# A two-layer hybrid inference step: TensorE issues in the order of tracing in the RWKV mixer and in the last layer's first token group

## The chip, the cores and the metric

The kernel runs on one core of one Trainium2 chip. The metric is the device time of the program in microseconds (us). The engines are named as in the profile: PE is TensorE, DVE is VectorE, ACT is ScalarE, POOL is GpSimd, and SP issues most of the DMA transfers. Matrices are multiplied on PE into PSUM banks; the other engines read the banks and the on-chip buffers (SBUF).

## The reference

One inference step of a two-layer decoder with model width 1024. A prompt of 1024 tokens with 16 learned tokens ahead of it (1040 tokens), and 8 single decode tokens with states of their own, go through both layers:

```python
for i in range(2):
    hn = rmsnorm(h, norm_mix[i])
    out = conformer_conv(hn) if i % 2 == 0 else rwkv7(hn)
    h = h + out
    h = h + square(relu(rmsnorm(h, norm_mlp[i]) @ w_in[i])) @ w_out[i]     # 1024 -> 4096 -> 1024
y = rmsnorm(h, norm_final)
```

Layer 0 mixes tokens with a Conformer convolution, layer 1 with RWKV-7 time mixing of 16 heads of 64. Time mixing projects r, k, v and, through small bottlenecks, a decay w, a rate a and a gate g for each token, and then runs a recurrence over the tokens for each head, with a 64 x 64 state S:

```python
sa = einsum(S, -kk_t)
S  = S * w_t + outer(sa, kk_t * a_t) + outer(v_t, k_t)
y_t = einsum(S, r_t)
out = ((groupnorm(y) + sum(r * k * r_k) * v) * g) @ w_o
```

The outputs are y of the prompt and of the decode tokens and the layers' final states.

## The kernel before

**Layer 0** works on three token groups and is not touched by the change. **Layer 1's mixer** works on four token groups of 272, 256, 256 and 264 tokens (`for g in range(4)`, L1417), and each group goes through eight pairs `p` of heads (128 columns). For each pair `mixer_in` (L880) traces the projection of r (`pr`), the second halves of the bottlenecks (`l_g`, `l_w`, `l_a`), the projection of v (`pv`), and then the deferred `finish` of the pair before: transposes of v (`vt`), products of the tokens within 32-token blocks (`nn`, L998, written to DRAM as `d_n`) and the bonus (`pk`, L1014). Between them it traces the key projections (`pk`, `pn`) of the next group. A projection (L845) is 16 matmul records of the trace, which stand as 8 rows in the order of instructions: each fp32 matmul leaves two records.

**The recurrence** runs over 17 chunks: chunk 0 holds the 16 learned tokens, chunks 1 to 16 hold 64 tokens each, and chunks 1, 5, 9 and 13 are the first of the four token groups. `front(c)` prepares a chunk. Before chunks 0, 1, 5, 9 and 13 it calls `inverses`, which loads the products `d_n` as `ni`, inverts 32 x 32 triangular blocks for one or four chunks in 30 rounds of two VectorE instructions (L1127, L1128: `tt<-ni`, `ni<-ni,tt`), and stores them as `d_p`. Then it loads `xa` and `bk` (DRAM `d_ab`) and the inverses `p32`, lets PE form the products of all tokens of the chunk (`A`, L1168, four banks) and DVE mask them (L1175, L1176), and transposes `p32` into `x32` on DVE (L1182). `chunk(c)` then does, on PE, `gg` (L1206, 32 x 32 tiles), the transposes `bT` (L1229), `W` (L1236), `po` (L1206), `U` (L1252), `S` (L1261) and `Y` (L1268, L1271), with copies and small products on the other engines between them, and updates the state `sv`. `bk` has one buffer, `xa` two. So `gg` of chunk 0 waits for this chain: `nn` of the last pair, DRAM, 60 DVE instructions, DRAM, `x32`.

**How the two are woven.** While the mixer of a group is traced, `tick` is called at every pair and in the projections; each call gives a credit, and `advance` traces steps of the recurrence until the credit is used up; the steps' prices stand in a table (`RW`). So the place of a recurrence step in the *program* is set by these credits. The place in which an engine *issues* it is set by something else: the whole program is ordered by a planner, which runs the instructions through a time model of its own and for each engine takes, of those that its model holds ready, the first in program order. An engine then executes its instructions strictly in that order, each behind the semaphores it needs.

**The last layer's stage** handles three token groups of 328, 352 and 352 tokens. For the first, `mixer_out(0)` multiplies the gated output by w_o (`ps_oo`), and `mlp(1, [group 0])` does the MLP: `ps_in` and `out`, with `h` and `r` on DVE behind them. These dense matmuls are split in three (L187, L188, L189: high by high, high by low, low by high parts). Into this stage a `filler` weaves what is left of the recurrence (chunks 13 to 16), the decode tokens' step (`decode_step`: 16 rounds of nine DVE instructions) and `norm_gate`, which transposes and gates the recurrence's output. The second and third token groups follow, with the same MLP.

PSUM is shared by name: four banks for the dense matmuls, one for small sums, and three ("w") for all steps of the recurrence.

Of the kernel before, what the change touches and what calls it, by code (L numbers as in the profile page):

```python
# [28 lines left out]
NCH = 1 + SEQ // HS  # L29
# [10 lines left out]
GN_OF = [[i for i, (lo, n) in enumerate(GN) if a <= lo < a + w] for a, w in G2]  # L40
# [8 lines left out]
def hybrid_step(tc, x_prompt, x_sample, state_conv, state_shift, state_wkv, meta_tokens,  # L49
# [8 lines left out]
    nc = tc.nc  # L58
    ctx = ExitStack()
    with ctx:  # L60
# [308 lines left out]
        with ExitStack() as l0:  # L369
# [6 lines left out]
            actp = [pool(l0, f"actp0{i}", 1) for i in range(2)]  # L376
            residp = [pool(l0, "resid00", 1)]
# [253 lines left out]
            with ExitStack() as s:  # L631
# [3 lines left out]
                fill, rest = filler(8 * KT, ([ranked(CV0, conv(0)), ranked(CV0, ln_silu(0))], EARLY * (15 * KT // 2 + 2 + 2 * MW + KT)))  # L635
# [6 lines left out]
                for g in range(3):  # L642
                    nxt, tail = iter(()), ()
                    if g < 2:
                        if g:
                            acts.append(new_act(actp[1], "hn2", N0))
                        nxt, tail = filler(TX, ([transpose_x(g + 1, *acts[g + 1])], 4 + 2 * KT))
# [202 lines left out]
        def keys(g, fill):  # L850

            c0, n = G1[g]
            nm = lambda s, *a: f"{s}{g}" + "".join(f"_{x}" for x in a)
            mix = prep[g][0]
            act = [mix(2, k) for k in range(KT)]
            pn = bank(nm("pn"), "x")
            add_pn = lambda: None

            def to_pn(p, sq):
                return lambda: nc.tensor.matmul(pn[:, :n], head_sel(p), sq[:, :n], start=p == 0, stop=p == KT - 1)  # L860
            for p in range(KT):
                yield
                ps = proj(next(wrkv), act, n, nm("k", p), fill)
                k_ = pr.tile([P, N1], F32, name=nm("st", p), tag="st", bufs=2)
                nc.scalar.copy(k_[:, :n], ps[:, :n])
                nc.sync.dma_start(d_k[:, p, c0:c0 + n], k_[:, :n])
                sq = pr.tile([P, N1], F32, name=nm("sq", p), tag="rk", bufs=2)
                nc.scalar.activation(sq[:, :n], ps[:, :n], AF.Square, scale=vec("k_k", p))
                add_pn()
                add_pn = to_pn(p, sq)  # L870
            r16 = lorap.tile([P, N1], F32, name=nm("r16"), tag="lf")
            r16p = norm[g] = [lorap.tile([P, N1], F32R, name=nm("r16" + q), tag="r16" + q, bufs=2)[:, :n] for q in "hl"]
            add_pn()
            nc.vector.tensor_scalar(r16[:, :n], pn[:, :n], L2_EPS * L2_EPS, None, op0=ALU.max)
            nc.scalar.activation(r16[:, :n], r16[:, :n], AF.Sqrt)
            nc.vector.reciprocal(r16[:, :n], r16[:, :n])
            split(*r16p, r16[:, :n], nc.vector)
# [432 lines left out]
        def advance(wait, last):  # L1310

            st["credit"] += wait
            while st["credit"] > 0 and st["done"] < last:
                w = next(rec)
                if w is None:
                    break
                st["credit"] -= w
            st["credit"] = min(st["credit"], 0)
# [93 lines left out]
        def tick(g, slow):  # L1412

            advance(PACE[g] * slow, NCH - 1)
            next(ng0, None)

        for g in range(4):  # L1417
            if g == 0:
                for _ in prepare(0):
                    pass  # L1420
                for _ in keys(0, lambda: None):
                    pass
            mixer_in(g, lambda slow=1.0: tick(g, slow))
        carry["tail"]()
        advance(CHUNK_WAIT * NCH, NEED[GN_OF[0][-1]])
        for _ in ng0:
            pass
        ld.close()


        with ExitStack() as l1:
# [10 lines left out]
            def mixer_out(g, residp, actp, fill, add):  # L1442
                lo, n = G2[g]
                h1 = hl[g] = residp.tile([P, KT, cur["wide"]], F32, name=f"h1_{g}", tag="h")
                nc.sync.dma_start(h1[:, :, :n], d_h[:, :, lo:lo + n])
                z = new_act(actp, f"z{g}", cur["wide"])
                for p in range(KT):
                    t = tt(f"zr{g}{p}", "t1")
                    nc.sync.dma_start(t[:, :n], d_z[:, p, lo:lo + n])
                    split(z[0][:, p, :n], z[1][:, p, :n], t[:, :n], nc.vector)  # L1450
                for m in range(KT):
                    ps = dense(load_col(rwkv_w_o[0], m, f"wo{g}_{m}", nc.gpsimd), z, n, f"oo{g}_{m}", fill)
                    nc.vector.tensor_add(h1[:, m, :n], h1[:, m, :n], ps[:, :n])
                    add(m, h1[:, m, :n])
                    fill()
# [57 lines left out]
            def group(g, actp, hidp, sums):  # L1513
                n = G2[g][1]
                hv = hl[g][:, :, :n]
                return (g, hv, n, *mlp_in(actp, hv, n, 1, f"m1{g}", sums), hidp)
# [4 lines left out]
                                ([until(NCH - 1)], FA * CHUNK_WAIT * (NCH - 1 - st["done"])),  # L1521
                                ([decode_step(), norm_gates(GN_OF[1]), ng2], NGA))
            add, sums = sums_of(0)
            mixer_out(0, residp, actp, fill, add)
            mlp(1, [group(0, actp, hidp, sums)], 2, nc.gpsimd, nc.vector, fill)
            for _ in rest:
                pass
            lw.close()
            outp = pool(l1, "outp", 1)
            cur["wide"] = max(n for lo, n in G2[1:])  # L1530
# [55 lines left out]
```

## Time and profile before

| | us |
|---|---|
| three runs | 2887.63, 2895.84, 2894.62 |
| median | 2894.62 |
| profiled execution | 2896.42 |
| its span | 2894.7 |
| mean granted clock of PE | 0.971 of full speed |

The span is cut by events of the trace into: layer 0 up to the mixer's first projection, `pk_0`, at 1124.2 us; the mixer with chunks 0 to 12, to its last `nn` at 1838.5; the mixer output with chunks 13 to 16 and the decode step, to about 2028; the rest of group 0's MLP, to 2313.3; and groups 1 and 2, to the end. In a row of PE events the columns are start, duration, engine, line, operation, output and inputs by the program's names (chunk and pair numbers left out), the tile of the array in use (128*128 is the whole array), the output's shape, and how many records the row joins; in square brackets stands how long the engine idled before it and what ended that.

### The profile page before, as it was taken

Reading aid. Unit: us, or ns where it says so; the run is one execution under the profiler, and the core shown is the slowest. Engines: PE = TensorE matmul, PEld = TensorE weight load, DVE = VectorE, ACT = ScalarE, POOL = GpSimd, SP = SyncE. Lnnn points to the kernel's source line nnn. Section 1 sums busy time; section 2 is a strip of 40 time slices with the busy share of each in tenths; the row PEclk is TensorE's granted clock in tenths of the full one; section 3 lists DMA queues with packets and bytes.
Section 4 is the critical chain, followed back from the end, with each engine's and each line's share of the span. In section 5 each row is a group of like instructions: output and inputs, shape, how many; then the busy total and the mean of one; then the engine's idle time right before and its main releaser. Section 6 shows DMA issues by size and latency. Waiting matters only on the chain.

```text
span 2894.7 us, 51574 instructions
## 1 busy us (share of the span) xinstructions
PE 2781.4 (96%) x19594; PEld 2573.7 (89%) x19594; DVE 1785.7 (62%) x3618; ACT 1187.1 (41%) x2233; POOL 1436.8 (50%) x1983
## 2 busy tenths in 40 slices
PE   8999999999999899999999999879999999999998
PEld 8988999999999898777877877777779999999998
DVE  5999999994454544336765555597345654444444
ACT  5546444543454332333445444443234552222223
POOL 6677778887788772000100111365246883343432
PEclk9999999999999999999999999889899999999999
DMA  6563544454444643687767767854336642222211
GB/s 181 171 184 95 154 139 132 137 178 138 138 145 146 189 151 109 183 213 202 183 184 202 180 159 181 206 143 126 95 109 198 192 148 87 70 66 74 66 59 41
DMA packets 649654, 416.42 MB, mean 144 GB/s; under 512 B 126184, under 2 KB 600360, under 8 KB 649406
## 3 DMA queue, kind: packets, MB, share of 16 engines
q1 hardware_dynamic: 643164, 410.20, 50.3%
q10 hardware_dynamic: 6018, 2.89, 0.4%
q8 instruction: 155, 2.54, 0.4%
q14 instruction: 93, 0.76, 0.1%
q0 software_dynamic: 224, 0.03, 0.0%
HBM read 345.60 MB, written 68.37 MB: 143 GB/s over the span
## 4 chain that ended last, share of the span: by engine, by line
PE 75%; DVE 9%; POOL 6%; DMA 4%; issue 3%; ACT 2%; SPq 0%; DVEq 0%; ACTq 0%; POOLq 0%
PE out L187 7%; PE out L189 7%; PE out L188 7%; PE ps_in L187 7%; PE ps_in L189 7%; PE ps_in L188 7%; PE pk L845 4%; POOL wo_lo L162 3%; PE pr L845 3%; PE pv L845 3%; POOL wi_lo L162 2%; PE A L1168 2%; DVE cv L504 1%; PE U L1252 1%; PE ps_g L187 1%
## 5 line engine op out<-in xcount | busy, mean ns | idle before, releaser
L162 POOL TENSOR_TENSOR wo_lo<-wo_raw,wo_hi 128x256 fp32r<-128x256 f32 x736 | 565.3, 800 | 329.6 <-ACT wo_hi L157 301.6
L162 POOL TENSOR_TENSOR wi_lo<-wi_raw,wi_hi 128x256 fp32r<-128x256 f32 x640 | 489.0, 796 | 293.6 <-ACT wi_hi L157 253.0
L187 PE MATMUL out<-hh,wo_hi 128*128 128x352 f32 (+2 forms) x1536 | 507.2, 330 | 20.4 <-DVE r L327 9.0
L340 DVE TENSOR_TENSOR h<-h,out 128x352 f32<-128x352 f32 (+2 forms) x768 | 386.4, 510 | 220.4 <-PE out L189 219.9
L187 PE MATMUL ps_in<-m_h,wi_hi 128*128 128x352 f32 (+2 forms) x1536 | 502.4, 327 | 12.7 <-ACT m_h L269 12.1
L189 PE MATMUL out<-hl,wo_hi 128*128 128x352 f32 (+2 forms) x1536 | 497.8, 327 | 5.6 <-DVE hl L141 5.6
L188 PE MATMUL out<-hh,wo_lo 128*128 128x352 f32 (+2 forms) x1536 | 502.1, 327 | 0.0
L188 PE MATMUL ps_in<-m_h,wi_lo 128*128 128x352 f32 (+2 forms) x1536 | 501.2, 327 | 0.0
L189 PE MATMUL ps_in<-m_l,wi_hi 128*128 128x352 f32 (+2 forms) x1536 | 500.4, 326 | 0.0
L504 DVE SCALAR_TENSOR_TENSOR cv<-u,wdw,cv 128x352 f32<-128x352 f32 (+2 forms) x720 | 376.9, 573 | 0.7
L157 ACT CAST wi_hi<-wi_raw 128x1024 fp32r<-128x1024 f32 x160 | 168.0, 1050 | 399.9 <-PE out L189 191.7
L157 ACT CAST wo_hi<-wo_raw 128x1024 fp32r<-128x1024 f32 x184 | 192.9, 1050 | 321.6 <-PE out L189 158.4
L187 PEld LDWEIGHTS out<-hh,wo_hi 128*128 128x128 f32 x1536 | 293.7, 191 | 28.3 <-DVE h L340 11.0
L187 PEld LDWEIGHTS ps_in<-m_h,wi_hi 128*128 128x128 f32 x1536 | 292.4, 190 | 17.1 <-ACT m_h L269 12.5
L189 PEld LDWEIGHTS out<-hl,wo_hi 128*128 128x128 f32 x1536 | 292.9, 192 | 9.4 <-DVE hl L141 7.1
L188 PEld LDWEIGHTS out<-hh,wo_lo 128*128 128x128 f32 x1536 | 293.6, 191 | 2.9
L189 PEld LDWEIGHTS ps_in<-m_l,wi_hi 128*128 128x128 f32 x1536 | 292.3, 190 | 2.9
L188 PEld LDWEIGHTS ps_in<-m_h,wi_lo 128*128 128x128 f32 x1536 | 291.9, 190 | 3.0
L327 DVE SCALAR_TENSOR_TENSOR r<-ps_in,rs_m 128x352 f32<-128x352 f32 (+2 forms) x192 | 98.5, 515 | 263.7 <-PE ps_in L189 260.0
L141 DVE TENSOR_TENSOR hl<-s,hh 128x352 fp32r<-128x352 f32 (+2 forms) x192 | 140.4, 732 | 99.4 <-ACT hh L140 99.1
L329 ACT ACTIVATE s<-r 128x352 f32<-128x352 f32 (+2 forms) x192 | 93.9, 491 | 133.0 <-DVE r L327 132.8
L845 PE MATMUL pv<-mx,wv_raw 128*128 128x256 f32 (+2 forms) x512 | 124.9, 398 | 5.5 <-ACT rk L1029 5.5
(350 smaller groups left out, 4925.3 us busy)
## 6 DMA issues: line engine op xcount, KB each, us to landing
wi_raw<-in_w_mlp_in_dram SPq DMA_DIRECT2D x160, 512.0 KB
wo_raw<-in_w_mlp_out_dram SPq DMA_DIRECT2D x160, 512.0 KB
wk_raw<-in_rwkv_w_k_dram SPq DMA_DIRECT2D x32, 512.0 KB
wr_raw<-in_rwkv_w_r_dram SPq DMA_DIRECT2D x32, 512.0 KB
wv_raw<-in_rwkv_w_v_dram SPq DMA_DIRECT2D x32, 512.0 KB
d_ab<-ab SPq DMA_DIRECT2D x32, 512.0 KB
pg_raw<-in_conv_w_pw_dram SPq DMA_DIRECT2D x24, 512.0 KB
pa_raw<-in_conv_w_pw_dram SPq DMA_DIRECT2D x24, 512.0 KB
```

The lines of the kernel that those rows point to most:

```text
L141: eng_lo.tensor_sub(lo, src, hi.bitcast(F32))
L157: nc.scalar.copy(hi[:, :a * b], raw[:, :a * b])
L162: eng_lo.tensor_sub(lo[:, cs], raw[:, cs], hi[:, cs].bitcast(F32))
L187: nc.tensor.matmul(ps, w[0], act[0], start=first, stop=False)
L188: nc.tensor.matmul(ps, w[1], act[0], start=False, stop=False)
L189: nc.tensor.matmul(ps, w[0], act[1], start=False, stop=last)
L327: nc.vector.scalar_tensor_tensor(r[:, :n], ps[:, :n], 0.0, rs[:, :n], op0=ALU.max, op1=ALU.mult)
L329: nc.scalar.activation(s[:, :n], r[:, :n], AF.Square)
L340: nc.vector.tensor_add(hv[:, 4 * i + m, :], hv[:, 4 * i + m, :], ps[:, :n])
L504: nc.vector.scalar_tensor_tensor(acc[m][:, :n], ug[:, m, j:j + n], wdw[:, m, j:j + 1], acc[m][:, :n], op0=ALU.mult, op1=ALU.add)
L845: nc.tensor.matmul(ps[:, :n], w[:, k, :], act[k], start=k == 0, stop=k == KT - 1)
L1168: nc.tensor.matmul(ps[:, i * 2 * P:(i + 1) * 2 * P], bk[:, j + i, :], xa[:, j + i].rearrange("p q x -> p (q x)"), start=True, stop=True)
```

## The change

`tc.manual_schedule(engines={nc.tensor.engine})` takes PE out of the planner's hands: inside it PE's instructions are issued in the order in which the program traces them. The other engines are still ordered by the planner, so their orders shift too where PE's does. The change puts two pieces of the program inside it: the mixer's loop over token groups with all of the recurrence that is traced there, and the first token group of the last layer. Its lines after the first are moved by one or two against those of before.

```diff
@@ -1414,17 +1414,18 @@
-        for g in range(4):
-            if g == 0:
-                for _ in prepare(0):
-                    pass
-                for _ in keys(0, lambda: None):
-                    pass
-            mixer_in(g, lambda slow=1.0: tick(g, slow))
-        carry["tail"]()
-        advance(CHUNK_WAIT * NCH, NEED[GN_OF[0][-1]])
-        for _ in ng0:
-            pass
+        with tc.manual_schedule(engines={nc.tensor.engine}):
+            for g in range(4):
+                if g == 0:
+                    for _ in prepare(0):
+                        pass
+                    for _ in keys(0, lambda: None):
+                        pass
+                mixer_in(g, lambda slow=1.0: tick(g, slow))
+            carry["tail"]()
+            advance(CHUNK_WAIT * NCH, NEED[GN_OF[0][-1]])
+            for _ in ng0:
+                pass
         ld.close()
@@ -1521,10 +1522,11 @@
-            mixer_out(0, residp, actp, fill, add)
-            mlp(1, [group(0, actp, hidp, sums)], 2, nc.gpsimd, nc.vector, fill)
-            for _ in rest:
-                pass
+            with tc.manual_schedule(engines={nc.tensor.engine}):
+                mixer_out(0, residp, actp, fill, add)
+                mlp(1, [group(0, actp, hidp, sums)], 2, nc.gpsimd, nc.vector, fill)
+                for _ in rest:
+                    pass
             lw.close()
```

The rows below are the order of instructions on one engine: line, operation, output and inputs (a tile's name carries group, pair or chunk, and a running number that differs between the two programs), the output's shape, and how many equal ones follow each other.

PE around `gg` of chunk 0, in the mixer's first token group (`pr1_2`, `pv1_3` are projections of group 1, `pk2_0`, `pk2_2` of group 2). Before:

```order
L998 MATMUL nn1_2_14621<-ab1_2_14454 32x32 x16
L1014 MATMUL pk1_2_14640<-rk1_2_14452,hsum_12483 128x256
L740 MATMUL pb1_3_14644<-r16h1_13809,hspread_12509 128x256
L740 MATMUL pb1_3_14644<-r16l1_13810,hspread_12509 128x256
L1206 MATMUL gg0_14291<-x320_14274,no0_14171 32x32 x16
L1229 MATMUL bT00_14319<-ident_58,bk0_14166 128x128 x4
L1229 MATMUL bT01_14325<-ident_58,bk0_14166 128x128 x4
L845 MATMUL pk2_2_14664<-mx2_2_0_14064,wk2_2_raw_14351 128x256
```

The same place after:

```order
L1168 MATMUL A06_14268<-xa0_12564,bk0_14168 128x256 x2
L845 MATMUL pk2_0_14237<-mx2_2_6_14078,wk2_0_raw_13953 128x256
L845 MATMUL pk2_0_14237<-mx2_2_7_14080,wk2_0_raw_13953 128x256
L845 MATMUL pr1_2_14289<-mx1_0_0_13832,wr1_2_raw_13988 128x256
L845 MATMUL pr1_2_14289<-mx1_0_1_13834,wr1_2_raw_13988 128x256
L845 MATMUL pr1_2_14289<-mx1_0_2_13836,wr1_2_raw_13988 128x256
L1206 MATMUL gg0_14293<-x320_14276,no0_14173 32x32 x16
L1229 MATMUL bT00_14321<-ident_58,bk0_14168 128x128 x4
```

Before, `gg0` stands behind `nn` of pair 2 of group 1; now it stands within the r projection of that pair, five projection rows behind `A06`, and the rest of that projection stands behind it.

PE at `W` of chunk 15, in the MLP of the last layer's first token group (`out1_4_0_4` is a dense output bank). Before:

```order
L1236 MATMUL W15_22073<-sv_12560,xa1_12565 64x64 x6
L187 MATMUL out1_4_0_4_22138<-hh10_8_21527,wo1_0_4_1_hi_22131 128x328
L1236 MATMUL W15_22073<-sv_12560,xa1_12565 64x64
L188 MATMUL out1_4_0_4_22138<-hh10_8_21527,wo1_0_4_1_lo_22132 128x328
L1236 MATMUL W15_22073<-sv_12560,xa1_12565 64x64
L189 MATMUL out1_4_0_4_22138<-hl10_8_21528,wo1_0_4_1_hi_22131 128x328
```

The same place after:

```order
L189 MATMUL out1_4_0_3_22070<-hl10_8_21533,wo1_0_4_0_hi_22021 128x328
L1236 MATMUL W15_22078<-sv_12560,xa1_12565 64x64 x16
L1206 MATMUL po15_22100<-p3215_21598,gg15_21950 32x32 x16
L187 MATMUL out1_4_0_4_22143<-hh10_8_21532,wo1_0_4_1_hi_22136 128x328
L188 MATMUL out1_4_0_4_22143<-hh10_8_21532,wo1_0_4_1_lo_22137 128x328
```

Before, matmuls of `W` and of the MLP take turns one by one; now `W` and `po` follow each other whole, between two MLP matmuls.

DVE in the middle of chunk 0's inverse. Before:

```order
L1083 TENSOR_TENSOR ab1_1_14230<-wa1_1_14147,em1_1_14220 128x4x128
L1128 TENSOR_TENSOR ni0_13949<-ni0_13949,tt0_19_14019 32x19x12
L1127 TENSOR_TENSOR tt0_18_14022<-ni0_13949 32x234
L1128 TENSOR_TENSOR ni0_13949<-ni0_13949,tt0_18_14022 32x18x13
L1127 TENSOR_TENSOR tt0_17_14025<-ni0_13949 32x238
L1128 TENSOR_TENSOR ni0_13949<-ni0_13949,tt0_17_14025 32x17x14
L1127 TENSOR_TENSOR tt0_16_14028<-ni0_13949 32x240
```

The same place after:

```order
L1127 TENSOR_TENSOR tt0_17_14027<-ni0_13951 32x238
L1176 TENSOR_TENSOR nr0_14172<-A04_14260,m_ar_12469 128x256
L1175 TENSOR_TENSOR xa0_12564<-A06_14268,m_ar_12469 64x2x64
L1128 TENSOR_TENSOR ni0_13951<-ni0_13951,tt0_17_14027 32x17x14
L1127 TENSOR_TENSOR tt0_16_14030<-ni0_13951 32x240
L1175 TENSOR_TENSOR xa0_12564<-A06_14268,m_ar_12469 64x2x64
L1176 TENSOR_TENSOR nr0_14172<-A06_14268,m_ar_12469 128x256
L1128 TENSOR_TENSOR ni0_13951<-ni0_13951,tt0_16_14030 32x16x15
```

The masks of chunk 0's last `A` banks, which stood outside this stretch of the inverse, now stand within it, ahead of its second half.

## The prediction

> **What bounds the kernel now.** I read the page's busy shares and chain first, then windows by stage, then TensorE's row of events at the places where the change moves something. The profiled execution took 2896.4 us (span 2894.7), 1.8 us over the median of the three runs shown (2894.6); the sum is made against 2896.4.
>
> ```profile
> PE 2781.4 (96%) x19594; PEld 2573.7 (89%) x19594; DVE 1785.7 (62%) x3618; ACT 1187.1 (41%) x2233; POOL 1436.8 (50%) x1983
> PE 75%; DVE 9%; POOL 6%; DMA 4%; issue 3%; ACT 2%; SPq 0%; DVEq 0%; ACTq 0%; POOLq 0%
> 1124.00:1300.00 176.00, 171.03 (x995) 140.53 (x993) 59.96 (x135) 54.07 (x159) 10.15 (x33) 0.99 0.72 204
> 1300.00:1839.00 539.00, 512.57 (x5214) 421.92 (x5215) 321.17 (x787) 247.35 (x645) 60.11 (x131) 0.97 0.72 182
> 1862.00:2028.00 166.00, 149.71 (x1092) 125.80 (x1087) 143.39 (x308) 57.26 (x104) 89.40 (x106) 0.88 0.56 146
> 2028.00:2313.30 285.30, 283.28 (x1878) 242.22 (x1878) 148.14 (x282) 117.38 (x219) 157.50 (x196) 0.93 0.52 149
> ```
>
> TensorE carries the chain (75%). The last four rows (window, length, then busy us and count of PE, PEld, DVE, ACT, POOL, granted clock, DMA share, GB/s) are the stages that the change covers. The mixer runs from 1124 to 1839, the first token group of the last layer from there to 2313. In 1862 to 2028 VectorE is the fuller engine of the two (143 of 166 us). In 2028 to 2313 PE looks full, but "busy" is modelled, and its matmuls are few: 1878 in 285 us, where a plain stretch of the same layer does
>
> ```profile
> 2220.00:2240.00 20.00, 20.00 (x136) 19.99 (x135) 14.20 (x26) 11.49 (x21) 17.42 (x22) 1.00 0.72 213
> 2014.17 0.33 PE L1236 MATMUL W<-sv,xa 128*64 128x64 f32 x2
> 2014.43 0.42 PE L187 MATMUL ps_in<-m_h,wi_hi 128*128 128x328 f32 x1
> 2014.78 0.33 PE L1236 MATMUL W<-sv,xa 128*64 128x64 f32 x2
> 1450.02 1.15 PE L1236 MATMUL W<-sv,xa 128*64 128x64 f32 x32
> 1451.10 0.69 PE L1206 MATMUL po<-p,gg 32*32 32x32 f32 x32
> 2040.83 0.59 PE L1168 MATMUL A<-xa,bk 128*128 128x256 f32 x2
> 2041.08 0.50 PE L188 MATMUL out<-hh,wo_lo 128*128 128x328 f32 x1
> 2041.41 0.59 PE L1168 MATMUL A<-xa,bk 128*128 128x256 f32 x2
> 2070.00:2073.00 3.00, 3.00 (x13) 1.71 (x12) 0.00 (x0) 1.49 (x3) 0.00 (x0) 0.50 0.09 14
> ```
>
> 136 in 20 us, 0.147 us each. Alternating one MLP matmul with one small one of the recurrence (two records) takes 2014.78 - 2014.17 = 0.61 us; apart they take 0.15 and 2/32 of 1.08, 0.07. So each change between the whole array and a tile of it (128*64, 64*64, 32*32 in the rows) costs (0.61 - 0.22) / 2 = 0.19 us. Between two whole-array forms it costs nothing: A with an MLP matmul takes 0.58, and apart 0.43 + 0.15. Where this alternation is thickest the granted clock falls to 0.50, although no idle time is shown.
>
> **The last stage, 2028 to 2313.** What the stage's matmuls would take in runs:
>
> ```profile
> L187 PE MATMUL out<-hh,wo_hi 128*128 128x328 f32 x208 | 69.9, 336 | 2.0 <-DVE h L340 1.3 <-DVE r L327 0.4 <-ACT hh L140 0.3
> L189 PE MATMUL ps_in<-m_l,wi_hi 128*128 128x328 f32 x181 | 63.0, 348 | 0.0
> L1268 PE MATMUL Y<-sv,xa 128*64 128x64 f32 x96 | 12.7, 240 | 0.0
> ```
>
> Three lines each of the first two make about 1164 matmuls, 175 us at 0.15. Y (two lines), S, U and W are 448 records at 0.034 (15 us); A, gg, po, the transposes and the final state add about 18. That is 208 us of 285: 77 us go elsewhere. The order of before has 319 changes of tile form on PE in this stage, that of after 22, for the same work. 297 changes at 0.19 are 56 us; at 77/319 = 0.24, which takes in the lowered clock, 71. Between them I take 64, as the clock follows the alternation in the row above, and give 4 back for MLP matmuls that VectorE, in its own fixed order, makes wait (it has 148 us of work there, PE over 200): **-60, between -71 and -45**.
>
> **The mixer: waits that appear.** PE executes in order, so a group that isn't ready now holds the projections behind it. Which groups? `gg` of chunk 0 needs chunk 0's 32x32 inverses, and those need `nn` of pair 7, a trip through DRAM, 60 VectorE steps, and a second trip:
>
> ```profile
> 1317.72 0.46 PE L998 MATMUL nn<-ab 64*32 64x32 f32 x32
> 1331.83 0.19 DVE L1127 TENSOR_TENSOR tt<-ni 32x30 f32<-32x30 f32 x1
> 1347.04 0.40 DVE L1127 TENSOR_TENSOR tt<-ni 32x240 f32<-32x240 f32 x1
> 1361.32 0.18 DVE L1128 TENSOR_TENSOR ni<-ni,tt 32x30 f32<-32x30 f32 x1
> 1369.27 0.45 DVE L1182 STREAM_TRANSPOSE x<-p 128x256 f32<-128x256 f32 x1 [6.05 <-DMA p<-d_p]
> 1369.77 0.69 PE L1206 MATMUL gg<-x,no 32*32 32x32 f32 x32 [2.74 <-DVE x L1182]
> 1305.64 4.92 PE L1168 MATMUL A<-xa,bk 128*128 128x256 f32 x12 [5.67 <-DMA bk<-d_ab]
> 1333.81 3.62 PE L845 MATMUL pv<-mx,wv_raw 128*128 128x256 f32 x16
> 1337.26 0.38 PE L981 MATMUL vt<-ident,vv 128*128 128x128 f32 x2
> ```
>
> From `nn` to `gg` it took 52.0 us, filled with projections but for 2.7. A projection's 16 records are 8 rows of the order and take 3.45 us, 0.43 a row. In the order of after 59 rows of that width and a few small ones stand between `nn` and `gg`: 27 us. If the chain stays as long, PE waits 25 us. VectorE's other work inside the chain is about the same in both orders. The least: VectorE's order now puts the masks of A's last two pairs (A06) before the inverse's second half, so 32 steps (0.43 us each at first, 0.21 at last, 10.6 in all) and the last 8.4 us (1361.3 to 1369.8) come after A06, with only 2.2 us of PE rows there: at least 17. I take **+26 (17 to 30)**. The same again for the other groups of four chunks:
>
> ```profile
> 1709.40 0.45 PE L998 MATMUL nn<-ab 64*32 64x32 f32 x30
> 1755.53 0.19 DVE L1128 TENSOR_TENSOR ni<-ni,tt 128x30 f32<-128x30 f32 x1
> 1766.31 0.69 PE L1206 MATMUL gg<-x,no 32*32 32x32 f32 x32 [1.48 <-DVE x L1182]
> 1485.41 0.46 PE L998 MATMUL nn<-ab 64*32 64x32 f32 x32
> 1559.09 0.45 DVE L1182 STREAM_TRANSPOSE x<-p 128x256 f32<-128x256 f32 x1 [6.17 <-DMA p<-d_p]
> 1415.34 0.45 DVE L1182 STREAM_TRANSPOSE x<-p 128x256 f32<-128x256 f32 x1 [3.97 <-DMA p<-d_p]
> ```
>
> Chunk 9: 56.5 us needed, 29 us of rows between, so about 27; the least, by the inverse's tail as above, 16: **+25 (16 to 28)**. Chunk 5: 73.7 us, but VectorE had mixes and gates of other chunks within, half of which its order now puts elsewhere; rows for 58: **+5 (0 to 16)**. Chunk 1: 46 us after chunk 0 (1369.7 to 1415.8), rows for 46: **+1 (0 to 3)**. The waits of before at these places go (5.67 for A, now 20 us later, 2.74, 1.48): **-10**. While PE stands, the queues on SP and POOL bring weights ahead, so a wait such as
>
> ```profile
> 1566.68 6.67 PE L845 MATMUL pv<-mx,wv_raw 128*128 128x256 f32 x16 [5.53 <-ACT rk L1029]
> 1300.00:1305.00 5.00, 0.00 (x0) 0.00 (x0) 1.75 (x1) 2.39 (x4) 0.00 (x0) 0.80 1.24 196
> 1305.00:1310.00 5.00, 4.36 (x11) 3.56 (x12) 0.29 (x1) 0.20 (x1) 0.00 (x0) 0.51 0.45 174
> ```
>
> (laid to ACT, which had long been done; a weight tile is likelier) mostly goes: **-4 (-8 to 0)**. After a stop the clock restarts low (0.51 for 5 us, 2.4 lost): two long stops and small ones, **+4 (0 to 7)**. Changes of tile form fall from 295 to 159 in the mixer; 136 at 0.19 are 26 us, and at about half that, since many stand between two small groups that follow without a gap (W and po above), 14: **-19**. The other steps of a chunk are further apart than they need (after po 4.5 to 8.5 us of rows, after U 4.3 to 7); for stray waits of half a us in each of 12 chunks **+6 (0 to 25)**. The mixer comes to 26+25+6-10-4+4-19+6 = **+34**.
>
> **Between, 1839 to 2028.** The inverses of chunks 13 to 16 and the decode step stand on VectorE, and its rows are nearly the same in both orders: no gain where it is the bound. PE's matmuls there come to some 118 us by the rates of the rows above. Nothing, between -15 and +15 (the mixer output's matmuls wait for z behind the inverses).
>
> **Sum:** 34 + 0 - 60 = -26, so 2870 us. All low ends together give 2803, all high ones 2940.
>
> **Rivals.**
> A. The stops in the mixer are not four but one in each chunk: A waits for `bk`, whose load can start only when `bT` has read the single buffer. The shortest distance in the trace is 8.4 us, in chunk 1: from l_a, which follows the last matmul of bT, to A:
>
> ```profile
> 1417.62 0.60 PE L943 MATMUL l_a<-la,wa 128*128 128x256 f32 x2
> 1426.06 1.10 PE L1168 MATMUL A<-xa,bk 128*128 128x256 f32 x4 [0.38 <-DMA bk<-d_ab]
> ```
>
> The new order gives it 11 to 14 us; if loads queued ahead on SP make it 16, 12 chunks cost 4 us each, 48 instead of the 6: 2912, slower. It decides from about 2.7 us a chunk on.
> B. The last stage becomes VectorE's: late `h` additions hold PE's banks and half of the 60 is lost: 2900, no change. For it, in 1862 to 2028 it was so; against, 148 us of VectorE's work in 285.
> C. VectorE is freer while PE stands, so the stops are at their least (33 instead of 51, and none at chunks 1 and 5) and the stage between gains 15: 2831.
> D. The alternation is not what costs the 77 us, as weight loads run ahead under any neighbour; then only the mixer's stops show. 34 + 19 without its gain in form changes: 2949, slower. The 0.61 us pair speaks against it. The Trainium skill, "TensorE: Matmul & The Clock Gate", section "Back-to-back issue gap", says that the spacing of a stream is set by both weight load and matmul, pipelined through a 64-deep window, some 81 ns for 128 columns. By that (an estimate of that page) a pair would take about 0.31 us and the last stage would gain some 14 us, 2916; the trace's pair takes twice that, so the sum goes by the trace.
>
> **Chances.** The forecast's case 0.50 (2850 to 2888), C 0.14, B 0.14, A 0.17, D 0.05. Of these the forecast's case is all but 0.02 faster, C faster, B half same and half slower, A and D slower; 0.3% (8.7 us) is about what a measurement of this kernel can tell. Faster 0.61, same 0.10, slower 0.29. The range 2828 to 2925 takes in C and A, and leaves out D and the ends of the bounds, some 0.17. The likeliest case alone has 2850 to 2888.
>
> **What would show it.** PE idle of 17 to 30 us before `gg` of chunks 0 and 9, released by VectorE's x32, with little at chunk 5 and none at chunk 13; W, U, S and Y in runs of 32 everywhere; the stage after the decode step near 225 us at a clock near 1. I am wrong if PE idles before A in every chunk, if that last stage stays over 260 us, or if the distance from 1124 to the mixer's last `nn` (715 us now: 176 + 539 of the windows) doesn't grow.

## The result, and the profile after

The changed kernel takes 2884.0 us against 2895.2 us before (medians of eight runs each): ratio 0.9968, 95% interval 0.9953 to 0.9984, so 5 to 14 us less, where 26 were forecast. The time lies in the predicted range and the sign is right; the size is less than half of the forecast's. The profiled execution took 2880.8 us (span 2878.8), 15.6 less than the one before it that the sum was made against.

The busy line and the chain's first line of the page after:

```profile
PE 2674.6 (93%) x19594; PEld 2528.6 (88%) x19594; DVE 1792.9 (62%) x3618; ACT 1188.9 (41%) x2233; POOL 1428.5 (50%) x1983
PE 74%; DVE 13%; DMA 6%; issue 2%; ACT 2%; POOL 1%; SPq 0%; ACTq 0%; DVEq 0%; POOLq 0%
```

PE is busy 107 us less for the same 19594 instructions, and only 16 us of that reach the end: it stands still 91 us more. The windows say where. Each row: window, length, busy us and count of PE, PEld, DVE, ACT, POOL, granted clock, DMA share, GB/s. Before, the mixer (from the first `pk` to the last `nn`), the mixer output (to the first `ps_in`), and the MLP of group 0:

```profile
1124.20:1838.90 714.70, 683.30 (x6208) 562.26 (x6206) 381.03 (x922) 301.39 (x803) 70.06 (x164) 0.98 0.72 187
...
1838.50:1917.80 79.30, 59.01 (x581) 51.76 (x580) 62.08 (x139) 30.45 (x57) 46.62 (x56) 0.83 0.79 198
1917.80:2313.90 396.10, 391.13 (x2602) 330.88 (x2603) 240.12 (x473) 157.92 (x291) 217.22 (x267) 0.92 0.51 146
```

The same three after:

```profile
1128.00:1880.80 752.80, 674.52 (x6305) 563.60 (x6303) 388.08 (x935) 305.58 (x810) 69.89 (x165) 0.95 0.68 177
...
1880.40:1958.90 78.50, 45.81 (x474) 41.63 (x475) 56.77 (x113) 31.96 (x55) 44.54 (x59) 0.76 0.82 215
1958.90:2295.60 336.70, 302.38 (x2612) 290.99 (x2610) 243.53 (x484) 152.71 (x285) 209.15 (x258) 0.95 0.60 169
```

The mixer is 38 us longer: PE busy 9 less, idle 47 more (31.4 to 78.3); 97 records more stand in it, since a chunk's last steps now come ahead of the last `nn`. The mixer output is as long as it was. The MLP is 59 us shorter: busy 88.8 less, idle 29.3 more (5.0 to 34.3). Layer 0, which the change does not touch, was 4 us longer in this execution; over the runs below it lies between 1122 and 1133 us.

PE's row of events shows the stops. In the mixer after, those that matter here (start, duration, what was issued, in brackets the idle time before it and its releaser):

```profile
1308.55 1.22 PE L922 MATMUL p_wa<-hx,wa_raw 128*128 128x256 f32 x2 [5.65 <-DMA wa_raw<-d_lr]
1367.41 1.06 PE L1206 MATMUL gg<-x,no 32*32 32x32 f32 x32 [16.91 <-DVE x L1182]
1483.56 1.09 PE L1388 MATMUL yn<-ident,ey 128*128 128x128 f32 x4 [6.68 <-DVE ey L1384]
1575.62 1.12 PE L1388 MATMUL yn<-ident,ey 128*128 128x128 f32 x4 [7.33 <-DVE ey L1384]
1666.80 0.71 PE L1388 MATMUL yn<-ident,ey 72*128 72x72 f32 x4 [2.87 <-DVE ey L1384]
1684.13 0.47 PE L1388 MATMUL yn<-ident,ey 72*128 72x72 f32 x4 [1.88 <-ACT uv L1254]
1786.97 1.07 PE L1206 MATMUL gg<-x,no 32*32 32x32 f32 x32 [13.33 <-DVE x L1182]
```

and in group 0's MLP the larger ones:

```profile
2091.75 0.63 PE L1388 MATMUL yn<-ident,ey 128*128 128x128 f32 x4 [3.93 <-issue]
2141.34 1.97 PE L1289 MATMUL pfs<-ident,fs 64*64 64x64 f32 x32 [3.21 <-DVE fs L1284]
2163.51 0.87 PE L1388 MATMUL yn<-ident,ey 96*128 96x96 f32 x4 [5.15 <-issue]
2187.40 0.66 PE L1388 MATMUL yn<-ident,ey 128*128 128x128 f32 x4 [2.88 <-DVE ey L1384]
2215.38 1.03 PE L1388 MATMUL yn<-ident,ey 128*128 128x128 f32 x4 [4.60 <-DVE ey L1384]
```

The two `gg` are those of chunks 0 and 9, which the prediction named. Where the bracket says "issue", the profile names no releaser. `yn`, the transposes in which `norm_gate` turns the normalised output of the recurrence, is in neither the sum nor the rivals.

### The profile page after: what moved, and what is told of

The parts are those of the page before. It is cut to its first block, busy times and chain, and to the rows that moved or that the text cites. A ratio compares the mean times of both kernels' runs of the same rounds, so it can differ in the third digit from the quotient of the medians.

```text
span 2878.8 us, 51580 instructions
## 1 busy us (share of the span) xinstructions
PE 2674.6 (93%) x19594; PEld 2528.6 (88%) x19594; DVE 1792.9 (62%) x3618; ACT 1188.9 (41%) x2233; POOL 1428.5 (50%) x1983
## 4 chain that ended last, share of the span: by engine, by line
PE 74%; DVE 13%; DMA 6%; issue 2%; ACT 2%; POOL 1%; SPq 0%; ACTq 0%; DVEq 0%; POOLq 0%
PE out L187 8%; PE ps_in L189 7%; PE ps_in L188 7%; PE ps_in L187 7%; PE out L188 7%; PE out L189 7%; PE pk L845 3%; PE pv L845 3%; PE pr L845 3%; DVE cv L504 2%; PE A L1168 1%; PE ps_o L189 1%; PE ps_oo L187 1%; PE ps_o L188 1%; PE ps_o L187 1%
## 5 line engine op out<-in xcount | busy, mean ns | idle before, releaser
L188 PE MATMUL ps_in<-m_h,wi_lo 128*128 128x352 f32 (+2 forms) x1536 | 494.6, 322 | 0.0
```

The source lines that it names most:

```text
L188: nc.tensor.matmul(ps, w[1], act[0], start=False, stop=False)
```

## The experiments

The times below are medians; a ratio is to the kernel before on the same chip in the same session, and where two runs of different sessions are compared, the us are the difference of their ratios times 2893. The stages are read from each run's trace as above: the mixer, and the last stage from the last `nn` to the last matmul of group 0's MLP. "Changes of form" counts, in the order of PE's instructions, how often a matmul of the whole array and one of a part of it follow each other: 260 in the mixer and 471 behind it before, 158 and 41 in the changed kernel.

| run | us | ratio (95%) | mixer | last stage |
|---|---|---|---|---|
| before | 2895.2 | 1 | 714.3 | 475.1 |
| changed | 2884.0 | 0.9968 (0.9953 to 0.9984) | 752.4 | 414.8 |
| e1_mixer_only | 2936.0 | 1.0156 (1.0142 to 1.0171) | 754.4 | 470.3 |
| e2_last_only | 2842.2 | 0.9823 (0.9811 to 0.9836) | 708.4 | 422.0 |
| e3_bt_run | 2890.5 | 0.9988 (0.9976 to 0.9999) | 753.0 | 420.0 |
| e4_bt_turns | 2914.0 | 1.0069 (1.0057 to 1.0081) | 779.9 | 421.1 |
| e5_yn_later | 2874.7 | 0.9940 (0.9927 to 0.9953) | 738.4 | 425.2 |
| e6_gg_later | 2865.0 | 0.9902 (0.9887 to 0.9917) | 716.5 | 436.1 |
| e7_last_yn | 2837.3 | 0.9812 (0.9797 to 0.9828) | 706.7 | 417.1 |
| e8_both_mended | 2850.9 | 0.9856 (0.9840 to 0.9872) | 701.3 | 440.1 |
| e9_last_less_dve | 2834.0 | 0.9798 (0.9773 to 0.9823) | 711.5 | 413.8 |
| e10_before_less_dve | 2887.2 | 0.9976 (0.9962 to 0.9991) | 715.9 | 464.5 |
| e11_mended_pace | 2864.3 | 0.9894 (0.9872 to 0.9916) | 720.5 | 429.7 |
| e12_last_pool | 2847.5 | 0.9824 (0.9797 to 0.9852) | 712.7 | 423.7 |
| e13_last_sq | 2807.1 | 0.9691 (0.9678 to 0.9704) | 708.2 | 389.0 |
| e14_last_yn_sq | 2816.5 | 0.9722 (0.9708 to 0.9735) | 710.6 | 394.7 |
| e15_after_sq | 2860.0 | 0.9869 (0.9852 to 0.9886) | 754.7 | 395.0 |
| e16_before_sq | 2909.2 | 1.0040 (1.0027 to 1.0052) | 712.9 | 482.3 |

**One block at a time.** From the changed kernel, one of the two regions is taken away.

```diff
 # e1_mixer_only
-            with tc.manual_schedule(engines={nc.tensor.engine}):
+            with ExitStack():
                 mixer_out(0, residp, actp, fill, add)
 # e2_last_only
-        with tc.manual_schedule(engines={nc.tensor.engine}):
+        with ExitStack():
             for g in range(4):
```

> Only the first block (the mixer) issues in the order of tracing on PE; the last layer's first token group stays with the planner. Theory (the two blocks add up, each as the two traces show it): the mixer grows by 38 us (from the first pk to the last nn 752 us instead of 714), and the rest stays near before, less about 6 us for 32 changes of tile form that its order happens to lose (471 to 439 at 0.19): 2895 + 32 = 2927, between 2918 and 2936. Rival (the mixer's loss is partly paid back later whatever the second block does, because chunks that come later find other work to hide them): 2900 to 2915.

> Only the second block (the last layer's first token group) issues in the order of tracing; the mixer is the planner's as before. Theory (the blocks add up): the stretch from the mixer's last nn to the end of group 0's MLP falls from 475 us by 58 as in the changed kernel, so 2895 - 58 = 2837, between 2828 and 2848, and PE shows about 40 us of idle time more than before in that stretch while its busy time falls by about 100. Rival (the last stage gains only because the mixer, being late, has left it a different mix of work): above 2860.

The first costs 43 us (2936.0 against 2892.9 in its session), at the upper edge of what was expected and far from the rival; the second gains 51, as expected. Together that is -8, and the changed kernel has -9 by its ratio. The blocks add up: the change is a gain and a loss of nearly the same size, and half of it alone is five times as good as the whole.

**The price of a change of form.** The control moves the transposes `bT` ahead of the `W` loop; the second kernel lets them take turns. PE's work is the same in both. Only the lines that come in are shown; the loop over `bT` behind `gg` goes, and its copies to SBUF follow the new loops.

```diff
 # e3_bt_run
+            bT = [bank(f"bT{c}{h}", "w") for h in range(2)]
+            for p in range(KT):
+                nc.tensor.transpose(bT[p // 4][:, p % 4 * P:(p % 4 + 1) * P], bk[:, p, :], ident)
             for p in range(KT):
                 for q in range(2):
                     nc.tensor.matmul(ps[HALF[q], ...], xa[:, p, q, :HS], sv[:, p, q, :], start=True, stop=True)
 # e4_bt_turns
             for p in range(KT):
+                nc.tensor.transpose(bT[p // 4][:, p % 4 * P:(p % 4 + 1) * P], bk[:, p, :], ident)
                 for q in range(2):
```

> The changed kernel with the eight transposes bT of each chunk moved from behind gg to just ahead of the W loop, whole and in one run; same work, nearly the same count of changes of tile form. It is the control of the next kernel. Both theories: within 10 us of the changed kernel's 2884 (bk is read some us later, so A of the next chunk may wait a little).

> As the control, but bT and W take turns: one transpose (whole array), two matmuls of W (128*64), and so on. By the orders that is 238 more changes of tile form than the control, and nothing else moves. Theory (each change costs 0.19 to 0.24 us): 45 to 57 us slower than the control; a little less where PE stood idle anyway. Rival (changes of form cost nothing or next to it, and the gain of the last stage came from another order of its waits): within 10 us of the control.

PE's row of events at chunk 1, in runs (e3_bt_run):

```profile
1419.83 1.04 PE L1231 MATMUL bT<-ident,bk 128*128 128x128 f32 x8
1420.79 1.15 PE L1234 MATMUL W<-sv,xa 128*64 128x64 f32 x32
1421.88 0.69 PE L1206 MATMUL po<-p,gg 32*32 32x32 f32 x32
```

and in turns (e4_bt_turns):

```profile
1425.61 0.34 PE L1233 MATMUL W<-sv,xa 128*64 128x64 f32 x4
1425.87 0.33 PE L1231 MATMUL bT<-ident,bk 128*128 128x128 f32 x1
1426.13 0.34 PE L1233 MATMUL W<-sv,xa 128*64 128x64 f32 x4
1426.40 0.33 PE L1231 MATMUL bT<-ident,bk 128*128 128x128 f32 x1
```

In runs, eight transposes take 0.96 us and 32 records of W 1.09, so one and four take 0.12 + 0.14 = 0.26; in turns they take 1426.13 - 1425.61 = 0.52. That is 0.13 us a change, where MLP matmul and W showed 0.19: the price hangs on the neighbours. The 168 added changes in the mixer should then cost 22, and the mixer grew by 27 (0.16 each). The 70 added in the last stage made it 1 us longer: PE's busy time there grew by 9 and its stops fell by 8. So the price is real (the rival with no price falls), but the rows suggest that it adds nothing to the time where PE would otherwise have stopped. By medians the two kernels differ by 24 us, less than the 45 to 57 expected. The control itself is 6 us slower than the changed kernel, within the 10 expected.

**The stops in the mixer.** The first kernel gives `yn` of the first token group three more ticks, the second gives `gg` of chunks 0 and 9 more projections to stand behind.

```diff
 # e5_yn_later, in norm_gate, ahead of the yn transposes
                 yield 2.5
+                for _ in range(3):
+                    yield 0
 # e6_gg_later, at the end of front(c)
-            yield RW[2]
+            yield RW[2] + {0: 18, 9: 16}.get(c, 0)
```

> The changed kernel with the yn transposes of the mixer (norm_gate of the first token group) traced three ticks later, about 7 us of projections, so that DVE has the normalised rows ready. In the changed kernel PE stands 6.7 + 7.3 + 2.9 + 1.9 = 18.8 us before them. Theory (stops of PE add up): these stops go and the time falls by 15 to 19 us, to about 2867 from 2884. Rival (something else, VectorE or a load, ends the mixer at the same time and the stop only moves to the next group in the row): less than 6 us faster.

> The changed kernel with gg of chunks 0 and 9 traced later, by 18 and 16 credits, so that some 19 and 18 us more of projections stand between the last nn and gg (47 and 64 us by the order instead of 28 and 30). Theory: the stops of 16.9 and 13.3 us before these gg go; but chunk 11 no longer fits into the mixer and its 6 us of matmuls move to the last stage. From the first pk to the last nn 752 falls to about 717; the last stage grows by 6 to 15; 2884 becomes 2857 to 2866. Rival (the recurrence that comes later in the last stage is what that stage waits for, through VectorE): the last stage grows by 25 or more and the time stays within 8 us of 2884.

With `yn` later the mixer falls by 14 us, of the 18.8 of its stops there, and the last stage of that execution was 10 longer; 8 us by the ratios remain, about half of the expectation and more than the rival's. With `gg` later the mixer falls by 36 and the stop at chunk 0 from 16.9 to 3.9, at chunk 9 to nothing. About half of the 36 is PE's work of chunk 11, which then stands in the last stage; that stage grows by 21, more than the 6 to 15 expected; net 19 us.

**The stops in the last stage.** The same for `yn` there, alone and with the two others:

```diff
 # e7_last_yn (from e2_last_only): the credits of norm_gate's steps
-                yield 3      # after the load of y
+                yield 2
-                yield 2      # after the squares
+                yield 1
-                yield 2.5    # ahead of the yn transposes
+                yield 6
-                yield 2.5    # after the store of z
+                yield 1
 # e8_both_mended: the changed kernel with the edits of e5, e6 and e7
```

> Only the last block in the order of tracing (2842), and in norm_gate more work between the normalising and the yn transposes (prices 2, 1, 6, 1 instead of 3, 2, 2.5, 2.5, the same sum). PE stood 3.5 + 7.5 + 5.6 + 4.7 = 21 us before yn in that kernel. Theory (stops add up): 15 to 21 us faster, 2821 to 2827. Rival (VectorE is the bound of that stage): within 8 us of 2842.

> Both blocks in the order of tracing, with the three edits of the runs before together. Theory: 2884 - 17 (yn in the mixer) - 22 (gg, net) - 15 (yn in the last stage) = 2830, between 2822 and 2842. Rival (waits pass on to the next group): 2855 or more.

The first is a miss: 3 us by the ratios, as the rival had it, and PE's stops before `yn` are still 20 us. Tracing `yn` later doesn't help if what it waits for comes later too. The three mends together give 32 us, the sum of the single ones (8, 19, 3) within the intervals: 2851, between the 2830 of the theory and the 2855 of its rival, as the third mend gave so little. The mixer is 701 us, shorter than the planner's 714, but a chunk more stands in the last stage. The rows about one of the stops of e7_last_yn, from DVE, ACT, PE and SP's queue in turn:

```profile
2113.67 0.68 DVE L1381 TENSOR_REDUCE ems<-eq 96x8 f32<-96x512 f32 x1 [4.81 <-ACT eq L1376]
...
2114.96 0.69 DVE L1384 TENSOR_TENSOR ey<-ey,ems 96x512 f32<-96x512 f32 x1
...
2113.01 0.63 ACT L1376 ACTIVATE eq<-ey 96x512 f32<-96x512 f32 x1 [4.46 <-DMA d_z<-ez]
...
2115.74 0.87 PE L1388 MATMUL yn<-ident,ey 96*128 96x96 f32 x4 [7.42 <-issue]
...
2101.22 2.68 SPq L1380 DMA_DIRECT2D ebv<-d_bv  x1
2104.00 1.98 SPq L1396 DMA_DIRECT2D d_z<-ez  x1
```

Read upwards from PE: `yn` starts at 2115.74, just as `ey` ends (2114.96 + 0.69), though the profile names no releaser; DVE's `ey` waits for the sums `ems`, these for ACT's square `eq`, and the square for a store: `d_z<-ez`, the gated rows of the half before, issued at 2104.0 behind other transfers of SP's queue. The square and the gated rows share one buffer (tag `eq`).

**Is it VectorE?** Rival B of the prediction had VectorE hold the stage. Seven of the nine instructions of a decode round are left out, in e2_last_only and in the kernel before.

```diff
 # e9_last_less_dve, e10_before_less_dve
-                    nc.vector.tensor_mul(t4, S, overv(2))
-                    nc.vector.tensor_reduce(sa[:, vs], t4, axis=AX.X, op=ALU.add)
-                    nc.vector.tensor_mul(S, S, overv(0))
...
-                    nc.vector.tensor_add(S, S, t4)
                     nc.vector.tensor_mul(t4, S, overv(4))
                     nc.vector.tensor_reduce(yd[:, vs], t4, axis=AX.X, op=ALU.add)
```

> Only the last block in the order of tracing (2842), and the decode tokens' state step left out but for two of its nine DVE instructions a round (the decode tokens' new state and their outputs are not computed): about 60 us less work on VectorE between the mixer and the end of group 0's MLP, none less on PE. Theory (with PE's 100 us of changes gone, that stage waits for VectorE in many places): 15 to 30 us faster, 2812 to 2827. Rival (the stage is still PE's, and its stops come from loads and from the order alone): within 6 us of 2842.

> The kernel before with the same seven instructions a round left out. Theory (before, PE with its changes of form filled that stage, and VectorE had room): at most 10 us faster, 2883 to 2893. Rival (VectorE bounded the first part of the stage before, as the prediction took it, so that nothing could be gained there by PE): 15 us or more faster. If both this and the last kernel gain alike, VectorE is as much of a bound before as after, and the give-back has another cause.

VectorE's busy time in the last stage falls by 50 us in the first (301 to 251) and 51 in the second (302 to 251). Both gain 7 us by their ratios, and the interval of the first overlaps that of e2_last_only. My theory of the first run, that VectorE is what the stage waits for, falls: it is as little of a bound after as before.

**Is it the shared buffer?** The squares of the last layer's gates go into a PSUM bank, and nothing else is changed:

```diff
 # e13_last_sq (from e2_last_only), e14_last_yn_sq (e7), e15_after_sq (changed), e16_before_sq (before)
-                y, bv, gt, sq = (cur[tag].tile(...) for tag in ("ey", "ebv", "egt", "eq"))
+                y, bv, gt = (cur[tag].tile(...) for tag in ("ey", "ebv", "egt"))
+                sq = cur["eq"].tile([P, KH * P], F32, name=f"eq{i}_{hf}", tag="eq") if i in GN_OF[0] else bank(f"eq{i}_{hf}", "x")
```

> Only the last block in the order of tracing (2842), and in the last layer's norm_gate the squares go into the PSUM bank for small sums instead of the buffer eq, which they share with the gated rows z that are stored to DRAM. Theory (in that kernel ACT's square waited 26 us in all for the store of the z before, 9 times, and VectorE and PE's yn behind it): PE's stops before yn fall from 22 us to under 8, and the time by 12 to 18, to 2824 to 2830. Rival (behind the store stands another wait, the load of y or VectorE's row): within 5 us of 2842.

> The same edit on the kernel whose yn is also traced later (2837, stops before yn still 20 us). Theory: with the buffer gone as a cause, the later yn now works, the stops fall to under 4 us: 2817 to 2823. Rival: within 5 us of 2837.

> The same edit on the changed kernel (2884; stops before yn in the last stage 18.5 us). Theory: 2868 to 2875. Rival: within 5 us of 2884.

> The same edit on the kernel before, where ACT's square waits as long for that store (22.9 us), but PE shows no stop before yn, since the planner put other matmuls there. Theory: no gain; the planner's order happens to take 36 more changes of tile form (507 for 471), some 5 us: 2890 to 2900. Rival (the wait costs the same under any order): 2875 to 2882.

The waits of ACT in the last stage (engine, output and line, what it waited for, us in all, times, longest), in e2_last_only:

```profile
ACT eq L1376 <- DMA d_z<-ez: 26.0, 9, 6.3
```

in the kernel before:

```profile
ACT eq L1376 <- DMA d_z<-ez: 22.9, 8, 7.5
```

and in e13_last_sq, where the wait for the store is gone:

```profile
ACT eq L1377 <- DVE ey L1376: 12.2, 11, 2.9
```

The window of group 0's MLP, from its first `ps_in` to its last matmul, in e2_last_only:

```profile
1921.60:2260.50 338.90, 302.95 (x2612) 291.38 (x2610) 242.15 (x484) 153.91 (x287) 209.74 (x259) 0.94 0.60 169
```

and in e13_last_sq:

```profile
1916.70:2226.30 309.60, 293.92 (x2613) 283.64 (x2612) 244.06 (x487) 154.64 (x288) 213.36 (x260) 0.98 0.66 184
```

PE's idle time there falls from 36 to 16 us, with no stop over 1.5 us before a `yn` any more, and its busy time by another 9 with the clock at 0.98 instead of 0.94. The window is 29 us shorter, the kernel 38 by the ratios, over twice the expectation. The changed kernel gains 29 from the same edit. The kernel before gains nothing and loses 12, though its square waited for that store nearly as long: the 48 records of `yn` in its MLP have no idle time before them, as its planner had put MLP matmuls ahead of and between them:

```profile
2082.08 0.32 PE L189 MATMUL out<-hl,wo_hi 128*128 128x328 f32 x1
2082.24 0.27 PE L1388 MATMUL yn<-ident,ey 128*128 128x128 f32 x1
2082.27 0.39 PE L187 MATMUL out<-hh,wo_hi 128*128 128x328 f32 x1
```

(With the edit its order has 36 more changes of form, and PE's busy time in group 0's MLP is 9 us longer; that these are the 12 us is not shown.) e14_last_yn_sq comes out at 2816.5, next to its theory's 2817 to 2823, but it is 9 us slower than e13_last_sq: with the buffer out of the way the later `yn` gains nothing more. The wait for the store was there all along; only with PE in a fixed order did it stop PE.

**Two that led nowhere.**

```diff
 # e11_mended_pace (from e8_both_mended)
-        PACE = [0, 2.0, 2.0, 2.0]
+        PACE = [0, 2.2, 2.2, 2.2]
 # e12_last_pool (from e7_last_yn)
-                    nc.vector.tensor_mul(S, S, overv(0))
+                    nc.gpsimd.tensor_mul(S, S, overv(0))
-                    nc.vector.tensor_mul(t4, overk(dq[:, 5, vs]), overv(1))
+                    nc.gpsimd.tensor_mul(t4, overk(dq[:, 5, vs]), overv(1))
```

> Both blocks in the order of tracing with the three mends (2851), and the credit of a tick in the mixer raised from 2.0 to 2.2, so that chunk 11 stands in the mixer again. Theory: the last stage loses the chunk's cost, 440 back to about 420, and the mixer gets its 6 us and a few us of stops at gg, as 42 us of rows instead of 47 and 65 stand behind nn: 2838 to 2846. Rival (it only moves the chunk): 2848 to 2856. In both the manual mixer gains nothing over the planner's, 2837.

> The kernel with the last block in the order of tracing and the later yn (2837), with two of the nine instructions of a decode round on GpSimd instead of VectorE. Some 18 us of VectorE's work go; GpSimd, which also prepares the MLP's weights (lo parts), gets about 30 us more. Theory (VectorE bounds the stage): 2 to 10 us faster. Rival (GpSimd's weights come late, or the round gets longer by the trips between the engines): 0 to 15 us slower.

A quicker pace brings chunk 11 back into the mixer and 10 us out of the last stage, but the stops at `gg` return (8.1 and 8.3 us) with two others, the mixer is 19 us longer, and the whole 11 slower than without it: outside both expectations. GpSimd in the decode step made the time neither clearly better nor clearly worse than e7's (intervals overlap).

The best kernel of these is e13_last_sq: the planner's order in the mixer, the order of tracing in the last stage, and the squares out of the shared buffer; 0.9691 (0.9678 to 0.9704) of before.

## Why the prediction was right or wrong

- **What failed.** -26 was forecast, -9 measured. Both regions left out one stream, the gates of `norm_gate`: PE stops at its transposes `yn` for 18.8 us in the mixer and 18.5 in the last stage. The terms that should have held them are "stray waits of half a us in each of 12 chunks" (+6) and "give 4 back for MLP matmuls that VectorE, in its own fixed order, makes wait". Tracing `yn` later in the mixer returned 8 us, and taking away the store that held it in the last stage 29.
- **The last stage, "-60, between -71 and -45", and the stretch ahead of it, "Nothing".** The trace has -60 for the two together and the block alone -51, but not where the prediction put it. Cut at the last instruction of the decode step, which ends at 2034.8 before (not about 2028) and at 2062.2 after, the two stretches are, before:

```profile
1838.90:2034.80 195.90, 172.66 (x1308) 145.91 (x1306) 156.46 (x335) 72.74 (x133) 107.30 (x129) 0.86 0.61 160
2034.80:2313.90 279.10, 277.08 (x1847) 236.37 (x1846) 145.34 (x276) 115.29 (x214) 156.53 (x195) 0.94 0.52 150
```

and after:

```profile
1880.90:2062.20 181.30, 139.29 (x1308) 129.55 (x1308) 156.28 (x331) 73.12 (x131) 106.10 (x133) 0.87 0.66 176
2062.20:2295.60 233.40, 208.44 (x1744) 202.63 (x1744) 144.01 (x265) 111.41 (x207) 147.59 (x184) 0.95 0.63 179
```

Behind the cut it is -46. PE's busy time falls by 69, of which some 8 is work that now stands ahead (an estimate: 29 MLP matmuls at 0.15, 64 small records at 0.034, 8 records of `A` at 0.22); that leaves 61 where 64 were forecast for the changes of form. But PE's stops rise by 23 (2.0 to 25.0) where 4 were to be given back: `yn` took 18.5, and the stops before `out`, MLP matmuls as the step meant, 6 in the whole MLP. Ahead of the cut it is -15, where the prediction took nothing because VectorE was the fuller engine: VectorE does the same 156 us of work there in a shorter time; PE's busy time falls by 33 and its stops rise by 19. From the first `ps_in` on there are 404 changes fewer, while the step counted 297, from 2028 on. So the -60 of the trace is luck: a gain that was not forecast covers most of the stops that were not.
- **The price of 0.19 to 0.24 us a change** held: PE's busy time in group 0's MLP fell by 88.8 us, and 88.8 / 404 = 0.22, with the lowered clock in it. For other neighbours it is 0.13 to 0.16. The Trainium skill, "TensorEngine Tiling (Array Packing)", section "Key Properties", says that a change of the tiling mode drains TensorE; the pairs in the traces agree (0.52 us in turns for 0.26 apart), and the page gives no time. Rival D, that changes cost next to nothing, is out.
- **The mixer, +34.** The trace has +38, the block alone +43, but the parts are others. `gg` of chunks 0 and 9 stopped PE for 16.9 and 13.3 us, at and below the low ends (17 and 16), not for the 26 and 25 taken: from `nn` to `gg` it took 48.5 and 45.5 us, not the 52.0 and 56.5 that the prediction kept from before. Why these chains were shorter was not tested. At chunks 5 and 13 there was no stop; 5 us had been taken for chunk 5. The "stray waits" of 6 (0 to 25) were 18.8 at `yn` alone. The gain by fewer changes, taken as 19, is 9 in the busy time, with the clock at 0.95 instead of 0.98 in it and a little more work. That the sum came near is luck again. The step that failed is the reading of the order by chunks: it followed the recurrence's own chain and left out the third stream that `tick` traces into the mixer, `next(ng0)`, the gates of the first token group.
- **Rival A** (a stop before `A` in every chunk) did not occur: the stops before `A` in the mixer are about 1 us or less. **Rival B** named the right place and the wrong engine: e9 took 50 us from VectorE and got 7. **Rival C**'s parts came true: the `gg` stops were 30 (it had 33), there was none at chunks 1 and 5, and the stretch between gained 15; its time, 2831, did not, as it kept the -60 and left out `yn` like the forecast. Whether its reason, a freer VectorE, is the right one was not tested.
- **The signs.** None of the signs of being wrong that the prediction had set appeared: no stop before `A` in every chunk, the stage behind the decode step at 233 us and not over 260, a longer mixer. They watched the terms that the sum had, not one that it lacked.
- **The sum.** +34 and -60 were each 9 us too good against the blocks measured alone (+43 and -51), and a difference of two such terms carries both errors whole: -26 forecast, -9 measured. The sum of traces (-16) is nearer than the medians only because the two executions lie on different sides of their medians.

## What to carry to other kernels

Fixing an engine's order can turn every wait of every stream in it into a stop of the whole engine: before doing it, list all streams traced into the region, each with the row it waits for and the rows that stand ahead of it, and not only the one the change is meant for. A wait that a planner hides by putting other work into it can cost nothing until the order is fixed: taking away the square's wait for a store through a shared buffer (23 us in all) gained nothing before and 29 to 38 us under the fixed order. So look in the list of waits of the *other* engines for those that end in a DMA through a buffer tag. Where a change touches two regions, do each alone: here one half was worth 51 us and the other cost 43.

## What the runs showed of the hardware

The price of a change between the whole array and a part of it is not one number: 0.19 us between a 328-column MLP matmul and W, 0.13 between a 128-column transpose and W. Changes between two parts of the array cost too where they come in turns; the counts above leave them out, and the prediction took small groups to follow each other without a gap. Where `Y` (128*64) and `gg` (32*32) take turns in the kernel before:

```profile
2063.98 0.24 PE L1206 MATMUL gg<-x,no 32*32 32x32 f32 x2
2064.15 0.33 PE L1271 MATMUL Y<-uv,nr 128*64 128x64 f32 x2
2064.41 0.24 PE L1206 MATMUL gg<-x,no 32*32 32x32 f32 x2
```

a pair takes 0.43 us; in runs, by the rows of W and `po` in e3_bt_run, two records of each form take 0.07 + 0.04, so a change is about 0.16. The trace of before has 35 such changes in group 0's MLP and that of after 5, which would be about 5 of the 88.8 us (an estimate, 30 at 0.16).

And a stop costs more than its idle time. About `gg` of chunk 0 in the changed kernel:

```profile
1350.00:1355.00 5.00, 0.50 (x3) 0.10 (x1) 4.66 (x13) 0.20 (x1) 0.00 (x0) 1.00 0.43 131
1355.00:1360.00 5.00, 0.00 (x0) 0.00 (x0) 4.55 (x14) 0.00 (x0) 0.00 (x0) 0.54 0.00 0
...
1365.00:1370.00 5.00, 2.59 (x40) 2.56 (x41) 1.73 (x7) 1.17 (x3) 0.00 (x0) 0.50 0.48 134
1370.00:1375.00 5.00, 5.00 (x20) 4.24 (x19) 4.49 (x16) 1.97 (x6) 0.00 (x0) 0.76 0.57 112
1375.00:1380.00 5.00, 5.00 (x80) 4.25 (x79) 4.76 (x12) 4.34 (x11) 1.04 (x2) 1.00 0.69 188
```

The granted clock halves some 5 us after PE stops (1350.5) and comes back only about 5 us after it starts again (1367.4). The Trainium skill, "TensorE: Matmul & The Clock Gate", section "Part 1: The HAM clock gate (the "warmup" mystery)", says that the clock falls after at least one idle window of about 3.4 us and returns after at least one busy one; the 5 us of the rows both ways do not contradict that. It fits that removing 20 us of stops in e13_last_sq also took 9 us off PE's busy time.
